# Long convolutions of a diffusion layer: full transforms by tables of both parities instead of radix 2, sums of absolute values on VectorE, and a fixed early order on TensorE

## The chip, the cores and the metric
The kernel runs on one core of one Trainium2 chip. The core's engines run their own instruction streams and wait for each other by semaphores: TensorE (PE; its weight loads are shown as PEld), VectorE (DVE), ScalarE (ACT), GpSimd (POOL) and SyncE (SP, which here only issues DMAs). The metric is the device time of one execution in microseconds; lower is better.

## What is computed
One layer of a diffusion backbone in float32: 512 latent tokens and 256 context tokens of width 1024. The part around the change is the Hyena branch, two long convolutions over the 512 positions with filters that a small network makes:

```python
def hyena_spectrum(n, w1, b1, w2, b2, w3, freq):
    ...
    h = jnp.sin(freq * (feats @ w1 + b1))
    h = jnp.sin(freq * (h @ w2 + b2))
    h = (h @ w3).reshape(n, 2, HY_ORDER, HY_W)
    ...
    filt = jnp.concatenate([h[:, 0], jnp.zeros((1, HY_ORDER, HY_W), f32), h[1:, 1][::-1]], axis=0)
    filt = filt / jnp.sum(jnp.abs(filt), axis=0, keepdims=True)
    return jnp.fft.rfft(filt, axis=0)

def hyena_mixer(u, sw, sb, spec, bias):
    u = short_conv(u, sw, sb)
    v, g1, g2 = jnp.split(u, HY_ORDER + 1, axis=-1)
    z = g1 * long_conv(v, spec[:, 0], bias[0])
    return g2 * long_conv(z, spec[:, 1], bias[1])
```

Before it, the modulation `c @ w_mod`, an RMS norm and the input projection `h @ w_in`; beside it attention and a Fourier branch; after it the merge of the three branches, routing, and 16 experts (SwiGLU, 64 tokens each), whose weights of 402 MB are the bulk of what is read.

## The kernel before
The kernel is written in a tile language. A planner orders the instructions of every engine by its own costs when the program is built, except in the stretch `early` (from L330 on), where `manual_schedule` keeps the order of the text on the engines that it names. The order on each engine is fixed in the program that runs. Values are kept in float32; for most matmuls a value is split into a high half (ScalarE copies it to the narrower format) and a low half (VectorE subtracts): `split`, L232 to 234. `mm3` (L227 to 230) multiplies two split values by three matmuls.

PSUM is given out as four buffers of 512 columns (`pmm`) and two pairs of them (`pbig`). Weights come through a ring of three 1 MB buffers (`load`, L224), issued on SP in order; a load waits until the matmuls on the buffer's old content are done.

The early stage (L330 to 513). SP loads the small network's weights, three of the eight tiles of `w_mod` (`wmods`), the decay table, x, the other five tiles as the ring comes free, then the context and the bias rows; GpSimd's queue loads the transform tables (`dfth`, `dftl`, L341; `invh`, `invl`, L598), which take half of the tile T2a. `mod1(kt)` is the modulation's matmul with tile kt into one PSUM buffer. `filt(t)` makes a quarter of the filters: matmuls, the product with the decay (L399), the split, absolute values on ScalarE (L405) in one buffer, and 16 matmuls per quarter that add them up in PSUM (`nsum`, L407). `xnorm` squares x on ScalarE (L380) and scales it on VectorE (L384). `spectra(f)` transforms the filters by planes (L228 to 230 with output `plane`; copies at L428, combinations L432 to 440), radix 2 over even and odd positions. `butterfly` (L448, L449) and `norms` (L502 to 512) finish the filters' spectra in `Gt`. The modulation row is copied at L486 and turned at L489. `need(idx)` splits a tile of `w_in`; `hT(i)` turns x and applies the modulation (L562, L564). The projections follow (`pj`, outputs `pmm`).

The convolutions (L644 to 870, 145 to 237 us in the trace). `forward` makes four half transforms of the tokens, odd and even positions apart, with 12 matmuls; ScalarE copies the odd ones (L653) and VectorE adds and subtracts (L655, L656) to give the planes `Zs` in SBUF. `pointwise(o, i)` multiplies both planes by the spectra (L666, L667), adds on VectorE for the real and mostly on GpSimd for the imaginary parts (L668, L669), undoes the radix 2 (L670, L671) and splits. The inverse transform of the first convolution takes 12 matmuls with 512 columns, that of the second, which gives channels by positions, 48 with 128 columns. Between them stand the projections 9 to 15 and the second part of the modulation (`mod2`, L790, 16 tiles through the same ring). In this part the planner orders all engines.

After the convolutions come attention with the rest of the projections as its filler, the merge, the routing (to about 560 us), and the experts, whose weights are prefetched into every buffer that comes free.

## Time and profile before

| | us |
|---|---|
| median of 3 runs | 1507.91 |
| lowest, highest | 1506.47, 1513.32 |
| the profiled execution | 1505.07 |
| its span, first to last instruction | 1503.3 |
| TensorE busy in the span | 1349.0 (90%) |
| VectorE busy | 514.5 (34%) |
| ScalarE busy | 286.2 (19%) |
| GpSimd busy | 134.7 (9%) |

The shares are averages over stages that have different limits, so the stages are read one by one, by windows of the trace. A row of the timeline gives the start, the length, the engine, the line of the kernel, the operation and the tiles (output <- inputs); in brackets the time that the engine stood idle before it and what ended that. Matmuls overlap: the distance of two starts, not the length, says what one costs.

### The profile page before, as it was taken

The page shows a single profiled execution, that of the slowest core. Times are in us where ns is not written, and L with a number is a line of the kernel's source. Part 1 is how long each engine was busy: PE and PEld are TensorE (multiplying, and loading weights), DVE is VectorE, ACT ScalarE, POOL GpSimd, SP SyncE. Part 2 cuts the span into 40 slices and gives each one's busy share as a digit, 9 for nine tenths or more (in the row PEclk, how much of TensorE's full clock was granted, in tenths as well). Part 3 has the DMA queues.
Part 4 walks back from the last instruction along what each step waited for, and adds up shares of the span by engine and source line. Part 5 has one row for each costly group of instructions (what it writes and reads, how often), then busy time and mean ns, then how long its engine had stood idle before and what let it go on. Part 6 is the DMA issues. An engine that isn't in the chain of part 4 may idle for free.

```text
span 1503.3 us, 16141 instructions
## 1 busy us (share of the span) xinstructions
PE 1349.0 (90%) x6681; PEld 718.5 (48%) x6681; DVE 514.5 (34%) x1010; ACT 286.2 (19%) x513; POOL 134.7 (9%) x128
## 2 busy tenths in 40 slices
PE   6899789999999889999999978979988989889896
PEld 3567458777788874433433423423423423423233
DVE  4676777667546471201211111101201201101123
ACT  4355224444433320100000000000000000000003
POOL 1033531000104110000000000000000000000002
PEclk8799899999999899999999999999999999999998
DMA  8414595311153766799999999999999999999994
GB/s 319 175 62 137 196 321 175 89 67 56 71 198 110 276 255 233 310 428 430 429 431 430 430 429 429 429 432 430 429 431 431 429 429 431 431 429 428 431 429 201
DMA packets 50371, 477.62 MB, mean 318 GB/s; under 512 B 5485, under 2 KB 10223, under 8 KB 16378
## 3 DMA queue, kind: packets, MB, share of 16 engines
q1 hardware_dynamic: 46008, 464.20, 75.1%
q0 software_dynamic: 2464, 8.00, 2.2%
...
q14 instruction: 21, 0.17, 0.0%
...
## 4 chain that ended last, share of the span: by engine, by line
PE 48%; DMA 39%; DVE 8%; ACT 2%; POOL 1%; issue 1%; SPq 0%; ACTq 0%; DVEq 0%; POOLq 0%
DMA rawT<-in_wu_dram 11%; DMA rawT3a<-in_wu_dram 9%; DMA rawwsp<-in_wg_dram 7%; PE py L1404 6%; PE pmm L228 6%; PE pmm L230 6%; PE pmm L229 6%; PE pu L1368 5%; PE pa L1368 5%; DMA rawT<-in_wd_dram 4%; PE gx L1339 3%; DMA rawT2a<-in_wg_dram 2%; DMA rawT2b<-in_wu_dram 2%; DMA rawwsp<-in_wu_dram 2%; PE pmm L1023 1%; PE pT L1010 1%
## 5 line engine op out<-in xcount | busy, mean ns | idle before, releaser
L1382 DVE TENSOR_TENSOR hid<-hid,pu 128x512 f32<-128x512 f32 x32 | 20.6, 684 | 455.6 <-PE pu L1368 443.2
L228 PE MATMUL pmm<-T,wsp 128*128 128x512 f32 x288 | 116.7, 408 | 4.2 <-ACT wsp L233 4.2
L230 PE MATMUL pmm<-T,wsp 128*128 128x512 f32 x288 | 114.6, 398 | 3.5 <-DVE wsp L234 3.5
L229 PE MATMUL pmm<-T,wsp 128*128 128x512 f32 x288 | 114.1, 396 | 0.0
L1381 ACT ACTIVATE hid<-pa 128x512 f32<-128x512 f32 x32 | 17.4, 594 | 419.6 <-PE pa L1368 405.2
L1324 POOL TENSOR_SCALAR vt<-iota,slot,rs 128x64 f32<-128x64 f32 x16 | 10.3, 669 | 735.5 <-PE stp L1419 717.0
L1339 PEld LDWEIGHTS gx<-vt,x 128*128 128x128 f32 x512 | 61.4, 193 | 29.3 <-issue 18.7
L1339 PE MATMUL gx<-vt,x 128*128 128x128 f32 x512 | 69.0, 287 | 5.2 <-DVE vt L1324 1.9
L1410 DVE TENSOR_TENSOR Y<-py,g2b 64x512 f32<-64x512 f32 x30 | 20.7, 689 | 152.6 <-PE py L1404 138.1
L234 DVE TENSOR_TENSOR wsp<-ld,wsp 128x1024 fp32r<-128x1024 f32 (+1 forms) x39 | 54.4, 1398 | 41.7 <-ACT wsp L233 41.6
L228 PEld LDWEIGHTS pmm<-T,wsp 128*128 128x128 f32 x288 | 54.7, 191 | 22.5 <-issue 7.0
L230 PEld LDWEIGHTS pmm<-T,wsp 128*128 128x128 f32 x288 | 54.8, 190 | 20.2 <-DVE wsp L234 5.0
L1404 PE MATMUL py<-rawT,hidT 128*64 128x512 f32 x224 | 50.6, 596 | 14.5 <-DMA rawT<-in_wd_dram 14.5
L1448 PE MATMUL sc<-Y,st 128*128 128x512 f32 (+1 forms) x128 | 57.0, 598 | 5.6 <-DVE Y L1410 5.6
L229 PEld LDWEIGHTS pmm<-T,wsp 128*128 128x128 f32 x288 | 55.0, 191 | 12.3 <-issue 1.7
L1390 ACT ACTIVATE hidT<-hp 128x512 f32<-128x512 f32 x16 | 9.6, 597 | 265.5 <-PE hp L1385 147.1
L233 ACT ACTIVATE wsp<-ld 128x1024 fp32r<-128x1024 f32 (+1 forms) x39 | 41.9, 1079 | 60.9 <-PE pmm L229 42.7
L1448 PEld LDWEIGHTS sc<-Y,st 128*128 128x128 f32 (+1 forms) x128 | 23.5, 189 | 39.5 <-issue 26.4
L1452 DVE TENSOR_TENSOR acc<-acc,sc 128x512 f32<-128x512 f32 x56 | 38.2, 686 | 10.9 <-PE sc L1448 10.9
L1404 PEld LDWEIGHTS py<-rawT,hidT 128*64 128x64 f32 x224 | 16.2, 137 | 48.6 <-issue 38.6
L1368 PE MATMUL pu<-rawT,xg 128*64 128x512 f32 x128 | 29.8, 597 | 9.8 <-DMA rawT<-in_wu_dram 9.8
L1368 PE MATMUL pu<-rawT,K1n 128*64 128x512 f32 x128 | 30.6, 599 | 6.8 <-DMA rawT<-in_wu_dram 6.8
(562 smaller groups left out, 2395.5 us busy)
## 6 DMA issues: line engine op xcount, KB each, us to landing
...
```

The lines of the kernel that those rows point to most:

```text
L228: mm(o, ah, bh, start=first, stop=False)
L229: mm(o, ah, bl, start=False, stop=False)
L230: mm(o, al, bh, start=False, stop=last)
L233: keep(A.activation(hi, src, AF.Copy))
L234: keep((eng or V).tensor_sub(lo, src, hi.bitcast(F32)))
L1339: mm(o[:, k % 4], x1[:, t, k * 128:(k + 1) * 128], oh[:, t], start=t == 0, stop=t == 3)
L1368: mm(ob[64 * hf:64 * hf + 64], xg[:, k, es_], w_[:, (2 * b + hf) * 512:(2 * b + hf + 1) * 512], start=k == 0, stop=k == 7)
L1382: V.tensor_mul(hid[:, bs], hid[:, bs], acc_[1][b] if e == NE - 1 else acc_[1][:, bs])
L1404: mm(o[64 * dh:64 * dh + 64, :], hcol(hT_, fb), w_[:, i * 1024 + dh * 512:i * 1024 + (dh + 1) * 512], start=fb == 0, stop=fb == 15)
L1410: V.tensor_mul(Y2[es2, dh * 512:(dh + 1) * 512], o[64 * dh:64 * dh + 64], M["g2b"][64 * dh:64 * dh + 64, dh * 512:(dh + 1) * 512])
L1448: mm(o, st[ks, t * 128:(t + 1) * 128], Y2[ks, ds_], start=True, stop=True)
L1452: V.tensor_add(acc[:, t, ds_], acc[:, t, ds_], o)
```

## The change
- **Tables.** The transform tables hold both parities: a second copy with the odd positions' sign turned (`e * [1, -1]`), so that each of the two planes f has its own table over all positions. The four tables grow from 256 KB to 512 KB each and fill T2a.
- **Transforms.** `forward(f)` makes plane f whole, by 12 matmuls that add even and odd positions in PSUM; its result stays in PSUM (two `pmm` buffers for plane 0, a `pbig` for plane 1). `pointwise(o, f, Z)` multiplies from there, for both halves i; the butterfly at its end is gone. `inverse(os_, f)` adds plane f's part of both outputs in PSUM, 12 matmuls per plane; the first plane's part is issued before the second plane's. The last inverse has 48 matmuls of 256 columns. `Zt` and the second T2b tile are gone. The filters' own spectra stay radix 2.
- **Absolute sums.** VectorE adds the quarters' absolute values in a tile `Fa`; `norms` sums over the partitions by two matmuls with ones and turns the result by four transposes. The `nsum` matmuls go.
- **Order.** `early` now covers TensorE too and reaches on to the first `need(0)`. Filters are made in the order 0, 2, 1, 3, between the modulation's matmuls, and the first two planes ahead of the last filter. win[0] is loaded right after the last tile of `w_mod`, ahead of the context. Half of x's scaling goes to ScalarE.

```diff
...
     e = np.stack([np.cos(ang), -np.sin(ang)], 2)
+    e = np.stack([e, e * np.array([1.0, -1.0])[:, None, None]], 3)
     c["dft_h"], c["dft_l"] = _split_const(e)
-    inv = e.transpose(3, 2, 1, 0) * (2.0 / 512.0)
+    inv = e.transpose(4, 3, 2, 1, 0) * (2.0 / 512.0)
     c["inv_h"], c["inv_l"] = _split_const(inv)
...
     Gt = hyg.tile([128, 2, 2, 2, 3, 256], F32, name="Gt")
-    dfth, dftl, invh, invl = (T2a[:, i, j].rearrange("p (a b f) -> p a b f", a=2, b=2) for j in (0, 2) for i in (0, 1))
+    dfth, dftl, invh, invl = (T2a[:, i, j:j + 2].rearrange("p a (b f n) -> p a b f n", b=2, f=2)
+                              for j in (0, 2) for i in (0, 1))
     B1 = cst.tile([128, 8, 2], F32, name="B1")
...
     early = scope()
-    early.enter_context(tc.manual_schedule(engines={ENG.SP, ENG.Activation, ENG.DVE}))
+    early.enter_context(tc.manual_schedule(engines={ENG.SP, ENG.Activation, ENG.DVE, ENG.PE}))
     packa = flat(E01)[:, :1667]
...
     wmods += [load(a["wmod"][kt * 128:(kt + 1) * 128, 0:2048]) for kt in range(3, 8)]
+    wst = {("ld", 0): load(a["win"][0])}
     xc = ep.tile([128, 2, 1024], F32, name="xc")
...
         for t in range(n):
-            V.tensor_scalar(xs[t0 + t], xs[t0 + t], r[:, t:t + 1], None, op0=OP.mult)
+            if t % 2:
+                A.activation(xs[t0 + t], xs[t0 + t], AF.Copy, scale=r[:, t:t + 1])
+            else:
+                V.tensor_scalar(xs[t0 + t], xs[t0 + t], r[:, t:t + 1], None, op0=OP.mult)
     Fh, Fl = ([flat(T3pair(x_, 2 * t)) for t in range(4)] for x_ in range(2))
     w3h, w3l = flat(T2b[:, 0, 1:3]), flat(T2b[:, 1, 0:2])
-    nsum = pmm("nsum")
+    Fa = ep.tile([128, 1024], F32, name="Fa")
     def filt(t):
...
         split(Ff, Fh[t], Fl[t])
-        Fa = flat(E10[:, 0:2])
-        A.activation(Fa, Ff, AF.Abs)
-        for b in range(8):
-            mm(nsum[:, b % 4:b % 4 + 1], Fa[:, b * 128:(b + 1) * 128], ones[:, 0:1], start=t == 0 and b == 0,
-               stop=t == 3 and b == 7)
+        if t:
+            Fb = flat(E10[:, 0:2])
+            A.activation(Fb, Ff, AF.Abs)
+            V.tensor_add(Fa, Fa, Fb)
+        else:
+            A.activation(Fa, Ff, AF.Abs)
     def plane(par, blk, dr, r):
         t = blk * 2 + par
-        mm3(o, dfth[:, par, r], dftl[:, par, r], Fh[t][:, dr * 512:(dr + 1) * 512], Fl[t][:, dr * 512:(dr + 1) * 512],
+        mm3(o, dfth[:, par, r, 0], dftl[:, par, r, 0], Fh[t][:, dr * 512:(dr + 1) * 512], Fl[t][:, dr * 512:(dr + 1) * 512],
             True, True)
...
         V.tensor_sub(hs_[os_, ns], h2_[gs], hs_[gs, ns].bitcast(F32))
-    early.close()
-    for kt in range(3):
-        mod1(kt)
+    mod1(0)
     filt(0)
+    mod1(1)
+    filt(2)
+    mod1(2)
     filt(1)
+    sp = spectra(0)
+    next(sp)
+    next(sp)
     mod1(3)
-    filt(2)
     filt(3)
-    mod1(4)
     xnorm(0, 4)
-    sp = spectra(0)
     for i in range(3):
         next(sp)
-        mod1(5 + i)
+        mod1(4 + i)
     drain(sp)
+    mod1(7)
     mrow = ep.tile([128, 512], F32, name="mrow")
...
     def norms():
-        nc_, ncol = (ep.tile([128, 4], F32, name=n) for n in ("nsc", "ncol"))
-        V.tensor_copy(nc_, nsum[:, :4])
-        V.reciprocal(ncol, nc_)
+        p_ = pmm("nsum")
+        for h in range(2):
+            mm(p_, ones, Fa[:, h * 512:(h + 1) * 512], start=h == 0, stop=h == 1)
+        V.tensor_mul(dbc, dbc, p_)
+        ns = ep.tile([128, 512], F32, name="mrow")
+        A.activation(ns, p_, AF.Copy)
+        p_ = pmm("ncol")
+        for b in range(4):
+            T.transpose(p_[:, b * 128:(b + 1) * 128], ns[:, b * 128:(b + 1) * 128], ident)
+        ncol = ep.tile([128, 4], F32, name="ncol")
+        V.reciprocal(ncol, p_[:, 0:512:128])
         V.tensor_tensor(sws, colp[:, C_SW + 8:C_SW + 24].rearrange("p (i j) -> p i j", i=4),
                         ncol[:, :, None].to_broadcast([128, 4, 4]), op=OP.mult)
-        dg = ep.tile([128, 1024], F32, name="dg", tag="Ft", bufs=3)[:, :512]
-        for b in range(4):
-            V.tensor_scalar(dg[:, b * 128:(b + 1) * 128], ident, nc_[:, b:b + 1], None, op0=OP.mult)
-        p_ = pmm()
-        mm(p_, ones, dg, start=True, stop=True)
-        V.tensor_mul(dbc, dbc, p_)
         G.tensor_add(Gt[:, :, 0, 0, 1, :], Gt[:, :, 0, 0, 1, :], v2(dbc))
-    wst = {}
     def need(idx):
...
         split(ht.rearrange("p (k n) -> p k n", k=2), hch[:, i:i + 2], hcl[:, i:i + 2])
+    early.close()
     need(0)
...
         return pb
-    def forward():
-        zo = pbig("planes")
-        ze = [pmm("plane") for _ in range(2)]
-        for par, zz in ((1, [zo[:, :512], zo[:, 512:]]), (0, ze)):
+    def forward(f):
+        Z = []
+        zb = pbig("planes") if f else None
+        for r in range(2):
+            z = zb[:, r * 512:(r + 1) * 512] if f else pmm("plane")
+            for m in range(2):
+                ms_ = slice(m * 512, (m + 1) * 512)
+                mm3(z, dfth[:, m, r, f], dftl[:, m, r, f], vh[:, ms_], vl[:, ms_], m == 0, m == 1)
+            Z.append(z)
+        return Z
+    def pointwise(o, f, Z):
+        for i in range(2):
             for r in range(2):
-                ps_ = slice(par * 512, (par + 1) * 512)
-                mm3(zz[r], dfth[:, par, r], dftl[:, par, r], vh[:, ps_], vl[:, ps_], True, True)
-        for r in range(2):
-            A.activation(Zs[1][r], zo[:, r * 512:(r + 1) * 512], AF.Copy)
-        for r in range(2):
-            V.tensor_add(Zs[0][r], ze[r], Zs[1][r])
-            V.tensor_sub(Zs[1][r], ze[r], Zs[1][r])
-    def pointwise(o, i):
-        for r in range(2):
-            e_ = G if r and (o, i) != (1, 1) else V
-            y = hyp.tile([128, 2, 256], F32, name="cvy", bufs=2)
-            for f in range(2):
                 t0 = hyp.tile([128, 512], F32, name="cv0", bufs=2)
                 t1 = hyp.tile([128, 512], F32, name="cv1", bufs=2)
-                V.tensor_mul(t0, Zs[f][0], flat(Gt[:, o, f, r, 1 - i:3 - i, :]))
-                V.tensor_mul(t1, Zs[f][1], flat(Gt[:, o, f, 1 - r, 1 - i:3 - i, :]))
+                V.tensor_mul(t0, Z[0], flat(Gt[:, o, f, r, 1 - i:3 - i, :]))
+                V.tensor_mul(t1, Z[1], flat(Gt[:, o, f, 1 - r, 1 - i:3 - i, :]))
+                e_ = G if r and (o, f, i) != (1, 1, 1) else V
                 e_.tensor_tensor(t0, t0, t1, op=OP.add if r else OP.subtract)
-                e_.tensor_tensor(y[:, f], t0[:, :256], t0[:, 256:], op=OP.add)
-            e_.tensor_tensor(y[:, 1], y[:, 0], y[:, 1], op=OP.subtract)
-            V.scalar_tensor_tensor(y[:, 0], y[:, 0], 2.0, y[:, 1], op0=OP.mult, op1=OP.subtract)
-            for m in range(2):
-                split(y[:, m], Yh[m][:, r, i * 256:(i + 1) * 256], Yl[m][:, r, i * 256:(i + 1) * 256], e_)
+                y = hyp.tile([128, 256], F32, name="cvy", bufs=2)
+                e_.tensor_tensor(y, t0[:, :256], t0[:, 256:], op=OP.add)
+                split(y, Yh[f][:, r, i * 256:(i + 1) * 256], Yl[f][:, r, i * 256:(i + 1) * 256], e_)
+    def inverse(os_, f):
+        for m in range(2):
+            for r in range(2):
+                mm3(os_[m], invh[:, f, r, m], invl[:, f, r, m], Yh[f][:, r], Yl[f][:, r], f + r == 0, f + r == 2)
     qscr = tc.dram_tile([64, 2, 8, 512], F32, name="qscr")
...
     g1t = hyp.tile([128, 1024], F32, name="g1t")
-    Zt = big2.tile([128, 2, 4, 512], F32, name="Zt", tag="T2b")
-    Zs = [[Zt[:, f, r] for r in range(2)] for f in range(2)]
-    forward()
-    pointwise(0, 0)
+    Z = forward(0)
+    pointwise(0, 0, Z)
     mod2(2)
     o = proj(9)
+    Z = forward(1)
     short_conv(uV1[:, 1], o, 3)
-    pointwise(0, 1)
+    pointwise(0, 1, Z)
     mod2(2)
             A.activation(g1t, to_tokens(uV1), AF.Copy)
+            oz = [pmm(), pmm()]
+            inverse(oz, 0)
         u_ = hyp.tile([128, 512], F32, name="uf", bufs=2)
...
         mod2(2)
+    inverse(oz, 1)
     for m in range(2):
-        o = pmm()
-        for r in range(2):
-            mm3(o, invh[:, r, m], invl[:, r, m], Yh[m][:, r], Yl[m][:, r], r == 0, r == 1)
         z = hyp.tile([128, 512], F32, name="zt")
-        V.tensor_mul(z, o, g1t[:, m * 512:(m + 1) * 512])
+        V.tensor_mul(z, oz[m], g1t[:, m * 512:(m + 1) * 512])
         split(z, vh[:, m * 512:(m + 1) * 512], vl[:, m * 512:(m + 1) * 512])
     o = proj(12)
-    forward()
+    Z = forward(0)
     short_conv(uG[:, 0], o, 4)
-    pointwise(1, 0)
+    pointwise(1, 0, Z)
     mod2(2)
     o = proj(13)
+    Z = forward(1)
     short_conv(uG[:, 1], o, 5)
-    pointwise(1, 1)
+    pointwise(1, 1, Z)
     mod2(4)
...
     q_stack(0, 1)
-    T2b = big2.tile([128, 2, 4, 512], F32R, name="T2b", tag="T2b")
     for c in range(2):
             cs_ = slice(i * 256 + c * 128, i * 256 + (c + 1) * 128)
-            for m in range(2):
-                os_ = slice(i * 256 + m * 128, i * 256 + (m + 1) * 128)
+            for f in range(2):
                 for r in range(2):
-                    mm3(o[:, os_], Yh[m][:, r, cs_], Yl[m][:, r, cs_], invh[:, r, m], invl[:, r, m], r == 0, r == 1)
+                    mm3(o[:, i * 256:(i + 1) * 256], Yh[f][:, r, cs_], Yl[f][:, r, cs_], flat(invh[:, f, r]), flat(invl[:, f, r]),
+                        f + r == 0, f + r == 2)
         z = hyp.tile([128, 512], F32, name="zt")
```

## Rows read from the trace of the kernel before
**Rows 1.** The page's chain that ended last, whole span, share by engine.
```profile
PE 48%; DMA 39%; DVE 8%; ACT 2%; POOL 1%; issue 1%; SPq 0%; ACTq 0%; DVEq 0%; POOLq 0%
```

**Rows 2.** The chain in order of time: start us, length us, what.
```profile
50.19 2.75 DVE xa L384 x4
...
187.10 1.85 PE pmod L790 x16
...
783.02 32.98 DMA rawT<-in_wu_dram
```

**Rows 3.** Windows: us, busy us of each engine (instructions), clock, DMA share, GB/s.
```profile
61.00:145.00 84.00, 79.75 (x374) 58.78 (x372) 58.69 (x82) 46.05 (x67) 26.20 (x19) 0.99 0.32 98
...
145.00:237.30 92.30, 77.44 (x397) 49.95 (x397) 72.63 (x116) 24.25 (x40) 35.46 (x32) 0.93 0.73 244
...
170.00:175.00 5.00, 0.00 (x0) 0.00 (x0) 5.00 (x8) 1.81 (x3) 2.10 (x3) 0.74 0.48 187
...
640.00:680.00 40.00, 38.65 (x177) 13.19 (x174) 3.35 (x5) 1.68 (x3) 0.00 (x0) 1.00 1.01 429
```

**Rows 4.** Who TensorE waited for, 145 to 237.3 us: us, times, longest.
```profile
PE pmm L228 <- ACT T3a L233: 8.6, 1, 8.6
...
PE pmod L790 <- DMA ld<-in_wmod_dram: 3.6, 3, 2.8
```

**Rows 5.** Timeline of TensorE: start us, length us, engine, line; neighbours' starts give the step.
```profile
90.28 0.28 PE L228 MATMUL pbig<-T2b,wsp 128*128 128x256 f32 x1
...
90.40 0.28 PE L229 MATMUL pbig<-T2b,wsp 128*128 128x256 f32 x1
...
90.52 1.02 PE L510 MATMUL pmm<-dg,ones 128*128 128x512 f32 x2
...
183.54 0.39 PE L228 MATMUL pmm<-T,wsp 128*128 128x512 f32 x1
...
183.77 0.39 PE L229 MATMUL pmm<-T,wsp 128*128 128x512 f32 x1
...
234.71 0.28 PE L229 MATMUL pmm<-T2a,T3b 128*128 128x128 f32 x1
...
234.82 0.27 PE L230 MATMUL pmm<-T2a,T3b 128*128 128x128 f32 x1
```

**Rows 6.** Groups on VectorE, 145 to 237.3 us: busy us, mean ns.
```profile
L666 DVE TENSOR_TENSOR cv<-Zt,Gt 128x512 f32<-128x512 f32 x16 | 13.7, 854 | 1.3 <-POOL cvy L669 1.3
...
L671 DVE SCALAR_TENSOR_TENSOR cvy<-cvy 128x256 f32<-128x256 f32 x8 | 3.9, 486 | 3.7 <-POOL cvy L670 3.6
...
L655 DVE TENSOR_TENSOR Zt<-plane,Zt 128x512 f32<-128x512 f32 x4 | 2.7, 688 | 1.0 <-PE plane L230 1.0
```

**Rows 7.** Timeline of VectorE and GpSimd side by side in the first convolution.
```profile
158.08 3.54 POOL L668 TENSOR_TENSOR cv<-cv,cv 128x512 f32<-128x512 f32 x1 [13.05 <-DVE cv L667]
...
159.46 0.68 DVE L667 TENSOR_TENSOR cv<-Zt,Gt 128x512 f32<-128x512 f32 x1
...
160.40 0.74 DVE L632 SCALAR_TENSOR_TENSOR uG<-pmm,sws,uG 128x511 f32<-128x511 f32 x1
...
167.35 1.21 DVE L666 TENSOR_TENSOR cv<-Zt,Gt 128x512 f32<-128x512 f32 x1
```

**Rows 8.** TensorE's group of absolute sums, 0 to 62 us.
```profile
L407 PE MATMUL nsum<-ones,E 128*128 128x1 f32 x64 | 10.6, 296 | 3.0 <-ACT E L405 3.0
```

**Rows 9.** Timeline of the early stage, 12 to 62 us.
```profile
18.51 2.36 DVE L399 TENSOR_TENSOR Ft<-pbig,E 128x1024 f32<-128x1024 f32 x2 [1.81 <-PE pbig L396]
...
32.58 1.23 DVE L234 TENSOR_TENSOR T3b<-Ft,T3b 128x1024 fp32r<-128x1024 f32 x1 [3.52 <-ACT T3b L233]
...
34.62 1.06 ACT L405 ACTIVATE E<-Ft 128x1024 f32<-128x1024 f32 x1 [2.08 <-PE nsum L407]
...
49.69 0.60 ACT L486 ACTIVATE mrow<-mod 128x512 f32<-128x512 f32 x1 [5.24 <-PE mod L362]
...
60.31 0.79 PE L230 MATMUL pmm<-T,wsp 128*128 128x512 f32 x1 [1.15 <-DVE wsp L234]
```

## The prediction
> **What bounds the kernel now.** First the page's chain that ended last [rows 1]: TensorE holds 48% of the span and DMA 39%. The chain in order of time says when [rows 2]: through TensorE and VectorE up to 783 us, from there mostly through the expert weights' DMA. The windows say why [rows 3]: from 640 us the DMA engines are busy all the time, at 429 GB/s, with a fixed amount of weights still to bring. Their buffers come free as TensorE works off the stages before. So a microsecond gained or lost on the path before 640 us moves the end by one, and what the change does after that is nothing. I therefore price two stages: the early one (0 to 62 us) and the two long convolutions (145 to 237.3 us).
>
> The second window of [rows 3] is the convolution stage: 92.3 us long, TensorE busy 77.4, VectorE 72.6. Neither is full, because they wait for each other: from 170 to 175 us TensorE does nothing at all while VectorE is busy throughout. The waits name the reason [rows 4]: 8.6 us in one piece for the last spectrum of the pointwise products (ScalarE's half of the split that VectorE feeds), and 3.6 us for modulation weights. After such a hole TensorE's steps are slow for some time. How much is lost altogether I get from the work at full clock. A 512-column matmul takes a step of 0.23 us, a 128-column one 0.11 [rows 5], a tile of modulation weights 0.93, with the gap behind it 1.0 [rows 2]. In the stage stand 7 projections of 24 (168 x 0.23 = 38.6), 16 modulation tiles (16.0), 24 forward (5.5), 12 first inverse (2.8), 48 short ones of the last inverse (5.3), 16 transposes (1.8): 70.0 us. 22.3 us are lost.
>
> **The convolutions, part by part.** Added on TensorE: each forward transform goes from 12 to 24 matmuls, twice (24 x 0.23 = 5.5); the first inverse from 12 to 24 (2.8); the last inverse keeps 48, but of 256 columns at 0.12 instead of 128 at 0.11 [rows 5] (0.5). Together +8.8, none of it hidden where TensorE is the bound.
>
> Removed on VectorE [rows 6]: 8 sums and differences of forward (L655 and L656, 8 x 0.69 = 5.5), 8 of L671 (3.9), and 5 of L670, which has their shape (5 x 0.49 = 2.4); 11.8 of 72.6 us. GpSimd loses 3 of L670. The count of products, L668, L669 and splits stays. The products now read the spectrum from PSUM: the PSUM-reading L655 takes 0.688 us [rows 6], a product left in peace 0.68 [rows 7], so I take zero; bounds: -0.17 each (L666's mean of 0.854 down to 0.688, 32 of them, -5.3 us) and +0.05 (+1.6).
> [...]
>
> More than sizes, the order changes. Plane 0's products need only forward(0), without the copies and butterflies, and inverse(oz, 0) needs only plane 0. TensorE has the projections 9 to 11, six modulation tiles, forward(1) and inverse(oz, 0), some 31 us, to lay over VectorE's two planes. The new balance is 70.0 + 8.8 = 78.8 us of TensorE against 61 us of VectorE. What stays lost: the stage from 61 to 145 us [rows 3] has a like balance (VectorE 58.7 beside TensorE 79.8 of 84.0) and TensorE idle 4.2 of it, 5%; 5% of 79 is 4.0; the 3.6 us for modulation weights stay (the ring of three loads isn't touched); some 0.9 for the clock after them. 8.5 in all. Bounds: 3.6 (the weights alone) and 22.3 (nothing goes). New stage: 78.8 + 8.5 = 87.3, **-5.0 us**, from -9.9 to +8.8. PSUM: plane 0's spectrum holds two of four "mm" buffers until its products are done, and plane 1's holds the free "big" pair, so to_tokens waits for plane 1's products. Behind that stand the g1t copy and the product zt, which need the last split anyway: zero, at most 2 us, inside the upper bound.
>
> **The early stage.** The 64 matmuls of absolute sums go: 10.6 us busy and 3.0 waiting [rows 8]. They share one buffer with ScalarE's absolute values, which wait for them in turn, 2.08 us before the last [rows 9]. That row of waits holds back the planes and the modulation matmuls behind it on TensorE; the modulation row is copied only at 49.7 [rows 9]. But in its place comes a row on VectorE, since all four engines now keep the program's order: per filter a product (about 1.2), ScalarE's high half (1.05), the low half (1.23 [rows 9]) and the sum of absolutes (about 1.23), one after another: 4.8 us. From the first product (18.5 [rows 9], and 2 later because the tables double, below) four filters end at 20.5 + 3.6 + 0.5 + 3 x 4.8 = 39.0. Then ScalarE squares x (four of 1.05 and their sums, 5), the reciprocal root and the scaling follow (4): x is scaled at some 47, where before it was at 53 [rows 2]. In the other strand the sixth plane waits for a PSUM buffer that ScalarE's copy or VectorE's first combination frees, and both stand behind that scaling; behind the plane stand the matmuls of modulation 5 to 7 and, by the ring, the load of win[0]; the ctx load and the bias rows stand behind that on SP (they have 20 us in hand). I get a modulation row at 52 to 55 in place of 49.7, win[0] split at 56 to 60, and projections that flow from 58 to 61; before, they flowed from 60.3, when the low half of the weights came [rows 9]. Value **-1.5 us**; bounds -6 (x alone decides) and +5 (the modulation row alone decides). The tables: four of 512 KB for 256 KB, so 1 MB more, which at the 429 GB/s of [rows 3] delays what queues beside them by up to 2.4 us, counted above.
>
> **The rest.** norms: two full-precision matmuls and four transposes for one matmul of 1.02 us [rows 5]: +0.5 to +1.5, or nothing if they land in an early hole of TensorE; +0.7. Half of x's scaling on ScalarE is inside the 4 us above; removing Zt frees no one.
>
> **Sum**: -5.0 - 1.5 + 0.7 = -5.8. The profiled execution took 1505.1 us (span 1503.3), so 1499.3; the median of the runs shown is 2.8 above that execution, so 1502 for the median.
>
> **Rivals.**
> A, the forecast (0.42): most of the wait goes, 1502; own range 1496 to 1508.
> B, everything goes (0.28): plane 0's inverse and forward(1) fill every hole, only the weights' 3.6 us stay, and early x decides: -9.9 - 4 = -14, so 1494. For it: VectorE and GpSimd hinder each other today. L668 on GpSimd took 3.54 us beside VectorE's products, and a product 1.21 beside GpSimd [rows 7]; which of the two is held up changes, as the product of 0.68 shows. The PSUM-reading L632 took 0.74 beside the same GpSimd instruction. With spectra in PSUM the 32 products would leave that conflict. Against: the adds and splits stay in SBUF.
> [...]
> C, no change (0.16): the hole only moves (TensorE's order in the convolutions is the planner's, and it may put to_tokens or the inverse too early again), about half of the 22 us stays and the early stage gives 5 back: 1506 to 1510.
> D, slower (0.14): the added 8.8 us fall on a TensorE that still ends its wait at the last split. Place: inverse(oz, 1) and the second forward pair. It decides from a remaining loss of 21 us on, near today's 22.3, and gives +8.8 + 0.7 and no early gain: 1517. Against it: VectorE has 12 us less to do before that split.
> That the change doesn't do what it says (plane 0's inverse issued only behind the last split) is a form of D or C.
>
> **How the numbers follow.** A measurement can tell about 0.5%, 7.5 us, from no change. Faster than 1500.4: B and the lower third of A, 0.40. Within: the rest of A and C, 0.46. Slower: D, 0.14. Range 1490 to 1514: it leaves out D and a little of B.
>
> **What would show it.** Convolution stage near 87 us, TensorE busy over 90% of it, the 8.6 us wait gone, VectorE's products at 0.69 with no long ones beside GpSimd; no absolute-sum matmuls; x scaled near 47 but the modulation row after 50; projections flowing near 59. The forecast is wrong if TensorE still stands for over 5 us before an inverse, if the early stage ends over 4 us from today's, or if the stages in between move.

## The result and the profile after

The changed kernel takes 1493.9 us (median; 1492.1 to 1495.6) against 1510.6 before (the three executions of the table and a fourth): ratio 0.989, 95% interval 0.986 to 0.992. Measured again later, on one chip with both, it is 1493.9 against 1509.9: 0.989 (0.988 to 0.991). The forecast of 1502, with its range from 1490 to 1514, had the sign right; its change of -5.8 us is about a third of that between the medians (-16.7). The profiled executions differ by less than the medians, 1505.1 us before and 1494.5 after, so -10.6; of that it is over half.

I cut each trace at two instructions that every kernel has: the first transpose of to_tokens (the convolutions start) and the first product with the fc weights (behind the last inverse). From the kernel before, and then from the changed one, TensorE's timeline (start us, length us, line, operation):
```profile
142.81 1.11 PE L640 MATMUL pbig<-packb,uT 128*128 128x128 f32 x8
...
245.12 0.36 PE L228 MATMUL pmm<-fc,T3b 128*128 128x256 f32 x1 [0.82 <-DMA fc<-in_fc_h_dram]
```
```profile
142.82 1.11 PE L650 MATMUL pbig<-packb,uT 128*128 128x128 f32 x8
...
235.28 0.35 PE L229 MATMUL pmm<-fc,T3b 128*128 128x256 f32 x1 [0.27 <-DMA fc<-in_fc_h_dram]
```
So in these two executions the early part is equal, the convolutions go from 102.3 to 92.5 us (-9.9), and what follows lasts 1258.2 and 1257.4. The chain that ended last has the same shape as [rows 1]:
```profile
PE 50%; DMA 41%; DVE 6%; ACT 2%; issue 1%; POOL 0%; SPq 0%; ACTq 0%; DVEq 0%
```
The same stretch as a window of each kernel (busy us of PE, PEld, DVE, ACT, POOL with their counts, then granted clock, DMA share, GB/s), before and after; the third row is after's counterpart of the convolution window of [rows 3]:
```profile
142.81:245.12 102.31, 85.99 (x439) 56.76 (x438) 77.86 (x124) 31.15 (x49) 39.44 (x38) 0.93 0.75 250
```
```profile
142.82:235.28 92.46, 89.72 (x476) 61.78 (x474) 66.79 (x100) 28.77 (x45) 34.83 (x38) 1.00 0.79 277
...
142.90:228.00 85.10, 82.62 (x445) 56.20 (x444) 63.91 (x96) 23.59 (x38) 32.58 (x34) 1.00 0.77 273
```
TensorE has more work and nearly no gap (2.7 us idle where it was 16.3), VectorE 11 us less, and the mean granted clock is 1.00 where it was 0.93. The 8.6 us wait of [rows 4] is gone. In this stretch TensorE waits for loads alone:
```profile
PE pmod L798 <- DMA ld<-in_wmod_dram: 2.5, 3, 1.7
PE pmm L229 <- DMA fc<-in_fc_h_dram: 0.3, 1, 0.3
```
Nor does the first inverse wait for its input any more. Its last split in the kernel before, then in the changed one, and there the start of the inverse of plane 0 and of that on the last split:
```profile
184.29 0.73 POOL L234 TENSOR_TENSOR T3a<-cvy,T3a 128x256 fp32r<-128x256 f32 x1
```
```profile
173.99 0.73 POOL L235 TENSOR_TENSOR T3b<-cvy,T3b 128x256 fp32r<-128x256 f32 x1 [0.53 <-ACT T3b L234]
...
174.66 0.48 PE L229 MATMUL pmm<-T3a,T2a 128*128 128x512 f32 x1
...
179.43 0.50 PE L229 MATMUL pmm<-T3b,T2a 128*128 128x512 f32 x1
```
With the same start of the stretch the last split ends at 174.7 and not at 185.0, 10.3 us earlier, and the inverse on it comes 4.7 us behind it. (The wait of 8.6 us before was for an earlier split of the same chain, done at 177.7.) In every trace of the old convolutions that split ends 41.7 to 42.2 us into the stretch, in every one of the new ones without an edit to them 31.9 to 32.3.

The products of VectorE, now from PSUM, are all near 0.68 us, where [rows 6] has 0.854 for L666 (groups: busy us, mean ns):
```profile
L673 POOL TENSOR_TENSOR cv<-cv,cv 128x512 f32<-128x512 f32 x7 | 9.8, 1404 | 31.6 <-DVE cv L671 31.6
...
L670 DVE TENSOR_TENSOR cv<-plane,Gt 128x512 f32<-128x512 f32 x8 | 5.5, 683 | 0.1
...
L671 DVE TENSOR_TENSOR cv<-planes,Gt 128x512 f32<-128x512 f32 x8 | 5.4, 676 | 0.0
```
The long products beside GpSimd are gone, but some of what still reads two SBUF operands got longer, as the low halves of the spectra's splits, before and after:
```profile
L234 DVE TENSOR_TENSOR T3a<-cvy,T3a 128x256 fp32r<-128x256 f32 x5 | 2.1, 414 | 0.0
```
```profile
L235 DVE TENSOR_TENSOR T3a<-cvy,T3a 128x256 fp32r<-128x256 f32 x4 | 3.6, 909 | 0.0
```
The early part after the change, beside [rows 9] (timeline):
```profile
43.88 1.42 DVE L390 TENSOR_SCALAR xa<-xa,xr 128x1024 f32<-128x1024 f32 x2
...
46.01 0.79 PE L229 MATMUL plane<-T3b,T2a 128*128 128x512 f32 x1 [10.35 <-DVE Gt L441]
...
54.15 0.60 ACT L495 ACTIVATE mrow<-mod 128x512 f32<-128x512 f32 x1 [7.12 <-PE mod L365]
...
60.52 0.50 PE L230 MATMUL pmm<-T,wsp 128*128 128x512 f32 x1 [1.31 <-DVE T L235]
```
x is scaled by 46 us and not by 53, but the sixth plane stands 10.35 us behind that scaling, the modulation row comes at 54.2 (49.7 before), and the projections flow from 60.5 (60.3 before).

All kernels by the two cuts, each read from the same two rows of its own trace ("rest" is the span less the second cut). Medians and ratios go over all timed executions. The kernel before was timed again beside each group, and its own median differs by 2 us between the groups; so where two kernels come from different groups, a distance of 2 us between their medians says nothing.

| kernel | to-tokens at | convolutions | rest | median | ratio to before (95%) |
|---|---|---|---|---|---|
| before | 142.8 | 102.3 | 1258.2 | 1508.6 to 1510.6 | 1 |
| before, again | 141.7 | 102.5 | 1258.3 | (1504.2) | |
| after | 142.8 | 92.5 | 1257.4 | 1493.9 | 0.989 (0.986 to 0.992) |
| after, again | 141.4 | 92.7 | 1258.0 | 1493.9 | 0.989 (0.988 to 0.991) |
| convolutions alone | 150.1 | 92.2 | 1257.8 | 1502.8 | 0.997 (0.995 to 0.998) |
| early half alone | 138.4 | 102.1 | 1257.6 | 1501.7 | 0.996 (0.995 to 0.998) |
| sums alone | 134.3 | 102.0 | 1259.1 | 1497.2 | 0.991 (0.990 to 0.992) |
| planes copied | 140.6 | 97.8 | 1258.1 | 1499.2 | 0.993 (0.990 to 0.996) |
| inverse late | 140.0 | 91.8 | 1257.8 | 1493.3 | 0.991 (0.989 to 0.993) |
| one term more | 141.0 | 95.6 | 1260.7 | 1497.3 | 0.992 (0.990 to 0.995) |
| modulation first | 143.1 | 92.6 | 1257.9 | 1495.3 | 0.993 (0.990 to 0.995) |
| TensorE kept busy | 139.0 | 92.7 | 1258.4 | 1492.1 | 0.989 (0.986 to 0.991) |
| planes first | 138.5 | 92.7 | 1257.2 | 1490.6 | 0.987 (0.986 to 0.988) |
| planes first, busy | 137.5 | 98.6 | 1258.0 | 1495.4 | 0.989 (0.988 to 0.991) |

### The profile page after: what moved, and what is told of

It is laid out like the page before. It is cut to its first block, busy times and chain, and to the rows that moved or that the text cites. A ratio compares the mean times of both kernels' runs of the same rounds, so it can differ in the third digit from the quotient of the medians.

```text
span 1492.7 us, 16055 instructions
## 1 busy us (share of the span) xinstructions
PE 1347.9 (90%) x6659; PEld 715.2 (48%) x6659; DVE 501.0 (34%) x981; ACT 287.8 (19%) x513; POOL 129.3 (9%) x128
## 4 chain that ended last, share of the span: by engine, by line
PE 50%; DMA 41%; DVE 6%; ACT 2%; issue 1%; POOL 0%; SPq 0%; ACTq 0%; DVEq 0%
DMA rawT<-in_wu_dram 11%; DMA rawT<-in_wd_dram 7%; DMA rawT3a<-in_wu_dram 6%; PE py L1410 6%; PE pmm L229 6%; PE pmm L230 6%; PE pmm L231 6%; PE pu L1374 6%; PE pa L1374 5%; DMA rawwsp<-in_wg_dram 5%; DMA rawwsp<-in_wu_dram 5%; PE gx L1345 2%; DMA rawT2a<-in_wg_dram 2%; DMA rawT2b<-in_wu_dram 2%; PE pmm L1029 2%; PE pT L1016 1%
## 5 line engine op out<-in xcount | busy, mean ns | idle before, releaser
L1330 POOL TENSOR_SCALAR vt<-iota,slot,rs 128x64 f32<-128x64 f32 x16 | 10.3, 670 | 735.5 <-PE stp L1425 716.8
L1416 DVE TENSOR_TENSOR Y<-py,g2b 64x512 f32<-64x512 f32 x30 | 20.7, 689 | 155.9 <-PE py L1410 141.4
L235 DVE TENSOR_TENSOR wsp<-ld,wsp 128x1024 fp32r<-128x1024 f32 (+1 forms) x39 | 54.5, 1406 | 41.5 <-ACT wsp L234 41.3
L231 PEld LDWEIGHTS pmm<-T,wsp 128*128 128x128 f32 x288 | 54.2, 188 | 16.1 <-DVE wsp L235 2.6
```

Source lines behind the costliest of these rows:

```text
L231: mm(o, al, bh, start=False, stop=last)
L235: keep((eng or V).tensor_sub(lo, src, hi.bitcast(F32)))
L1416: V.tensor_mul(Y2[es2, dh * 512:(dh + 1) * 512], o[64 * dh:64 * dh + 64], M["g2b"][64 * dh:64 * dh + 64, dh * 512:(dh + 1) * 512])
```

## The experiments

**The convolutions alone.** The forward, pointwise and inverse functions and their tables as in the change; the early half as before.
```diff
-    forward()
-    pointwise(0, 0)
+    Z = forward(0)
+    pointwise(0, 0, Z)
...
+    Z = forward(1)
...
+            inverse(oz, 0)
...
+    inverse(oz, 1)
```


> The convolution half of the change alone (full transforms by tables of both parities, products from PSUM, the inverse in two halves); the early half stays as before: sums on TensorE, the planner's order. Theory (the whole gain is made in the convolution stage and carried 1:1 to the end): the stage from 142.9 us to the mark that stood at 237.3 before and 228.0 after becomes 85 to 86 us (94.4 before), the profiled execution is 9 to 10 us under that of before, and the medians agree with the changed kernel within 3 us. Rival (the early half brings 5 to 6 us that the two profiled executions do not show, since the medians differ by 16.7 us and the profiled executions by 10.6): the stage is as short, but the median lies 5 us or more above that of the changed kernel.

1502.8 us, 5.8 under before. TensorE's timeline:
```profile
150.05 1.11 PE L642 MATMUL pbig<-packb,uT 128*128 128x128 f32 x8
...
242.27 0.36 PE L229 MATMUL pmm<-fc,T3b 128*128 128x256 f32 x1 [0.57 <-DMA fc<-in_fc_h_dram]
```
The convolutions are as short as in the changed kernel (92.2), so their gain is theirs alone. But the early part is 7 to 8 us longer than in either trace of before, although its code is the same but for the larger tables, and its instructions on TensorE come in the same order. Its timeline shows where that begins:
```profile
21.32 1.22 DVE L401 TENSOR_TENSOR Ft<-pbig,E 128x1024 f32<-128x1024 f32 x1 [4.61 <-PE pbig L398]
...
40.51 3.58 PE L409 MATMUL nsum<-ones,E 128*128 128x1 f32 x16 [1.21 <-ACT E L407]
...
55.28 2.74 DVE L386 TENSOR_SCALAR xa<-xa,xr 128x1024 f32<-128x1024 f32 x4
```
The first filter's product comes 2.8 us later than in [rows 9], as TensorE waited 2.1 us for early modulation weights (0.5 before) and then ran the filters at a granted clock of 0.87 and 0.70 (16 to 20 and 20 to 24 us; 1.00 in both before). The last row of sums starts 4.8 us later (35.73 before), and x is scaled 5.1 us later than in [rows 2]. So a small delay at the start grew along the sums. It starts with the 1 MB more of tables: the decay table, loaded beside them, lands 16.9 to 17.9 us after its issue in all ten traces with the larger tables and 14.8 to 15.2 in the four with the smaller ones. How much of the 7 to 8 us that is, no run with the tables alone tells. The rival held for the time: the changed kernel lies 8.9 us lower, nearly all of it ahead of to-tokens.

**The early half alone.** Fixed TensorE order, sums on VectorE, scaling shared, win[0] placed; the convolutions as before.
```diff
-    early.enter_context(tc.manual_schedule(engines={ENG.SP, ENG.Activation, ENG.DVE}))
+    early.enter_context(tc.manual_schedule(engines={ENG.SP, ENG.Activation, ENG.DVE, ENG.PE}))
...
+            V.tensor_add(Fa, Fa, Fb)
```


> The early half alone (TensorE order of the filters fixed by hand, absolute sums added by VectorE, two of the four x tiles scaled by ScalarE, win[0] loaded where the order puts it); the convolutions stay as before. Theory (the early half is worth nothing: the modulation row comes at 54 us instead of 49.7, and the projections start at 60.3 to 60.5 us either way): to-tokens starts at 142.5 to 143.5 us, the convolution stage stays at 94 to 95 us, and the median is within 2 us of that of before. My prediction's early step: -1.5 us, between -6 and +5. Rival (the early half holds the 6 us between the medians and the profiled pair): 5 us or more under before.

1501.7, 6.9 under before: my theory fell. To-tokens starts at 138.4, 3.3 and 4.4 us earlier than in the two traces of before. The sixth plane waits in this trace too:
```profile
44.16 0.79 PE L228 MATMUL plane<-T3b,T2a 128*128 128x512 f32 x1 [10.35 <-DVE Gt L439]
```
With the larger tables the same early half starts to-tokens at 140.0 to 142.8 in five traces (after, after again, planes copied, inverse late, one term more), 1.6 to 4.4 us later. So the early half is worth 6 to 7 us in the median with the smaller tables, although it has the hole.

**The sums alone.** The kernel before; only the absolute sums go from TensorE to VectorE.
```diff
-        for b in range(8):
-            mm(nsum[:, b % 4:b % 4 + 1], Fa[:, b * 128:(b + 1) * 128], ones[:, 0:1], ...)
+        if t:
+            Fb = flat(E10[:, 0:2])
+            A.activation(Fb, Ff, AF.Abs)
+            V.tensor_add(Fa, Fa, Fb)
```


> The kernel before, with one piece of the early half alone: the absolute sums added by VectorE and summed by two matmuls at the end, instead of 64 small matmuls beside the filters. TensorE's order stays the planner's, x is scaled by VectorE, win[0] is loaded as before, the convolutions are those of before. The whole early half gave 6.9 us in the medians. Theory (it is the fixed order that counts: filters, planes and modulation no longer interleaved with gaps at half clock): within 2.5 us of the kernel before. Rival (it is the sums: 10.6 us of TensorE at small matmuls, gone): 4 to 7 us under the kernel before.

1497.2, 12.7 under before in the medians (in the traces to-tokens comes 7.4 and 8.5 us earlier), and some 5 us under the whole early half: the theory that the order counts fell, and the rival was too low. One row of the kernel before, then the timeline of this one:
```profile
39.56 0.80 PE L228 MATMUL plane<-T3a,T2a 128*128 128x512 f32 x1 [0.25 <-DVE nsc L502]
```
```profile
39.91 2.73 DVE L384 TENSOR_SCALAR xa<-xa,xr 128x1024 f32<-128x1024 f32 x4
...
43.27 0.60 ACT L487 ACTIVATE mrow<-mod 128x512 f32<-128x512 f32 x1 [7.10 <-PE mod L362]
...
51.79 0.79 PE L230 MATMUL pmm<-T,wsp 128*128 128x512 f32 x1 [1.15 <-DVE wsp L234]
```
x is scaled by 42.6 (53 before, 46 after), the modulation row comes at 43.3 (49.7, 54.2), and the projections flow from 51.8 (60.3, 60.5). In the planner's order the planes and the modulation go on while x is squared. So the sums were the price of the old early part, in two ways that no run separates. They stood in TensorE's queue, waited for ScalarE (3.0 us, [rows 8]), and everything behind waited with them. And they held one of the four PSUM buffers to their end: before, the third plane waits for it until 39.56 (the row above), while here three planes are done by 27.5. The rest of the early half (fixed order, shared scaling, win[0]) takes some 5 us of that back on the old convolutions. The sums with the new convolutions and the planner's order weren't run; from the two parts (1497.2, and 9.9 us of convolutions) that is an estimated 1487, later by what the larger tables cost at the start.

**Modulation first.** The last 16 modulation matmuls ahead of the remaining planes.
```diff
+    mod1(4)
+    mod1(5)
+    mod1(6)
+    mod1(7)
     xnorm(0, 4)
-    for i in range(3):
-        next(sp)
-        next(sp)
-        mod1(4 + i)
     drain(sp)
-    mod1(7)
```


> The changed kernel, with the last four steps of the modulation (16 matmuls) put ahead of the remaining spectrum planes in TensorE's fixed order, so that they run while the planes wait for their PSUM buffers. Theory (the sixth plane waits 10.35 us behind the scaling of x, and the modulation, its row, the load of win[0] and its split are queued behind that plane; this is where the early half loses what it gains by the earlier scaling): the modulation row comes at 45 to 49 us (54.15 in the changed kernel), projections flow from 53 to 56 us (60.5), and the whole is 4 to 7 us under the changed kernel. Rival (the loads of the projections' weights, not the row, set when the projections can flow, or the planes that now come later hold up the Gt chain and the first conv): the row is early, but to-tokens starts within 1.5 us of 143.0, and the whole is within 1.5 us of the changed kernel.

1495.3, no better than the changed kernel: the rival held. The row came at 47.7 and the projections flow from 55.95 (60.5 in the changed kernel, after two single products at 57.6). But TensorE did nothing from 52 to 55.95 except its transposes, and what came then ran at half clock (windows):
```profile
52.00:56.00 4.00, 0.98 (x9) 0.74 (x7) 4.00 (x8) 1.07 (x4) 0.00 (x0) 0.93 0.18 29
56.00:62.00 6.00, 6.00 (x16) 4.49 (x17) 4.92 (x17) 2.40 (x3) 0.00 (x0) 0.50 0.39 157
```
By 62 us it had finished 10 products of the projections, the changed kernel 7, and by 70 us 34 against 33: the lead was nearly gone.

**TensorE kept busy.** 38 matmuls into an unread PSUM buffer where the sixth plane waits.
```diff
+    wm = pbig("warm")
     for i in range(3):
         next(sp)
+        if i == 1:
+            for _ in range(38):
+                mm(wm[:, :512], dfth[:, 0, 0, 0], Fh[0][:, :512], start=True, stop=True)
         next(sp)
         mod1(4 + i)
```


> The changed kernel, with 38 matmuls of 512 columns into a PSUM buffer that nobody reads, put into TensorE's order where the sixth spectrum plane waits (36 to 46 us, no matmul at all from 36 to 44 us, granted clock 0.78 then 0.50 until 52 us). 38 x 0.23 = 8.7 us at full clock, double that at half clock. Theory (the early half loses time because TensorE, after such holes, does its next work at half clock): the clock stays near 1.00 from 36 to 52 us, planes and modulation behind the hole take 4 to 5 us instead of 7, to-tokens comes 2 to 4 us earlier, the time is 2 to 4 us under the changed kernel. Rival (the stretch behind the hole waits for the x tiles and for win[0], whatever the clock): within 1 us of the changed kernel. Point against: if the extra matmuls run at half clock they end at 52 us, and all is 4 to 6 us later.

1492.1, by ratio and median 0.6 to 1.9 us under the changed kernel, within its interval, so between the theory's 2 to 4 and the rival's 1: the mechanism shows, and a gain in time isn't clear of the noise. Windows of the changed kernel, then of this one:
```profile
36.00:44.00 8.00, 0.00 (x0) 0.00 (x0) 4.42 (x15) 5.49 (x10) 0.00 (x0) 0.64 0.32 122
44.00:52.00 8.00, 5.99 (x17) 2.86 (x17) 3.44 (x5) 3.03 (x4) 2.50 (x2) 0.50 0.19 46
```
```profile
36.00:44.00 8.00, 8.00 (x37) 6.61 (x36) 4.15 (x13) 5.74 (x10) 0.00 (x0) 1.00 0.41 131
44.00:52.00 8.00, 6.06 (x36) 2.31 (x35) 4.41 (x8) 3.31 (x5) 2.52 (x2) 1.00 0.31 97
...
51.84 0.60 ACT L499 ACTIVATE mrow<-mod 128x512 f32<-128x512 f32 x1 [4.44 <-PE mod L365]
```
Without the hole the granted clock is 1.00 in both windows, 33 useful matmuls and the last 3 unread ones fit from 44 to 52 us where 17 did at 0.50, and the row comes 2.3 us earlier, though the plane could start no earlier (46.38 against 46.01).

**Planes first.** The remaining planes and the modulation ahead of the squares and the scaling of x.
```diff
-    xnorm(0, 4)
     for i in range(3):
         next(sp)
         next(sp)
         mod1(4 + i)
     drain(sp)
     mod1(7)
+    xnorm(0, 4)
```


> The changed kernel, with the whole rest of the first spectrum's planes and the modulation ahead of the squares and the scaling of x, on TensorE, VectorE and ScalarE. Theory (the sixth plane then no longer waits behind the scaling): no wait of 10 us on TensorE there, the modulation row at 42 to 46 us (54.15 in the changed kernel), x scaled 1 to 2 us later (47 to 48.5), projections from 51 to 55 us (60.5), and TensorE idle ahead of them, so that their first 5 to 8 us run at half clock: the time 1 to 4 us under the changed kernel. Rival (as in the run with the modulation first: all that is gained goes to the clock): within 1 us or up to 3 us over the changed kernel.

1490.6, 3.3 under the changed kernel beside it, as the theory had it (1 to 4), and the lowest median of the study; all its four executions lie under all eight of the changed kernel. The wait for the sixth plane is gone and x is scaled from 45.2, little over a microsecond later than in the changed kernel. TensorE is done with the modulation at 43.2, but the row is copied only at 47.32, as ScalarE has the squares and the scaling ahead of it (a miss of my 42 to 46). Projections from 53.1. The granted clock is 0.79 in the mean from 52 to 60 us; matmuls of 512 columns that follow each other step by 0.24 to 0.31 us up to 54.5, by 0.41 to 0.43 from there to 57.7, and by 0.23 to 0.24 from 59.3. So half clock came, but for an estimated 3 us (by these steps) and not the 5 to 8 that I expected:
```profile
47.95 1.11 PE L498 MATMUL pmm<-packb,mrow 128*128 128x128 f32 x4 [4.77 <-ACT mrow L495]
...
53.11 0.73 PE L229 MATMUL pmm<-T,wsp 128*128 128x512 f32 x2 [2.35 <-DVE ht L573]
...
52.00:60.00 8.00, 6.89 (x28) 5.38 (x29) 6.47 (x20) 2.40 (x5) 0.00 (x0) 0.79 0.49 198
```

**Planes first, and TensorE kept busy.**
```diff
     xnorm(0, 4)
+    wm = pbig("warm")
+    for _ in range(32):
+        mm(wm[:, :512], dfth[:, 0, 0, 0], Fh[0][:, :512], start=True, stop=True)
```


> As the run with the planes first, and 32 matmuls of 512 columns into a PSUM buffer that nobody reads (32 x 0.23 = 7.4 us at full clock) behind the modulation, where TensorE has nothing to do until x is scaled. Theory (the clock is what the order alone loses): granted clock 0.95 to 1.00 from 40 to 61 us, projections at full clock from their start, to-tokens at 133 to 137 us (142.8 and 140.0 in profiles of the changed early half), the time 4 to 7 us under the changed kernel. Rival (x or win[0] come last whatever the clock): within 1.5 us of the run with the planes first.

1495.4, worse than with the planes first. The early part did what was expected in kind (clock 1.00 from 40 to 61 us, to-tokens at 137.5, 1.1 us earlier than with the planes first and just outside the 133 to 137 expected). What was lost came later: the convolutions took 98.6 us. TensorE's waits in this stretch, then the window from 200 to 220 us here and with the planes first:
```profile
PE pmod L801 <- DMA ld<-in_wmod_dram: 6.5, 3, 3.7
...
200.00:220.00 20.00, 14.59 (x65) 8.57 (x58) 13.85 (x22) 3.08 (x6) 6.09 (x8) 0.83 1.01 289
```
```profile
200.00:220.00 20.00, 18.20 (x104) 12.31 (x105) 16.66 (x24) 4.66 (x8) 6.43 (x9) 1.00 0.96 305
```
The instructions of the stretch come in the same order in both kernels, but TensorE waited 6.5 us for modulation weights (2.3 with the planes first), with the DMA engines busy throughout at a lower rate (289 GB/s against 305), and the granted clock in that window was 0.83 against 1.00. Of this kernel's five executions two took 1490.5 and 1490.8 us, as with the planes first, and three 1495.4 to 1497.5: so it seems not to happen each time, though only one of them has a trace. Why the weights come late is open; neither theory covers it.

**Planes copied.** Each spectrum plane copied by ScalarE to SBUF ahead of its products.
```diff
+            A.activation(Zs[f][r], z, AF.Copy)
-            Z.append(z)
+            Z.append(Zs[f][r])
```


> The changed kernel, with each spectrum plane copied by ScalarE to SBUF (8 copies of 128x512) before the products, so that the 32 products of VectorE read SBUF instead of PSUM; order and TensorE work stay. The products took 854 and 813 ns from SBUF before and 676 to 683 ns from PSUM after; GpSimd's sum of them 1886 before and 1404 ns after. Theory (reading PSUM keeps VectorE's products out of the way of GpSimd, and that is what shortened both): products at 0.80 to 0.86 us, the GpSimd sum at 1.8 to 1.9 us, the stretch from to-tokens to the first fc product 2 to 5 us longer (92.4 after), the time 2 to 5 us over the changed kernel. Rival 1 (the products are shorter for another reason): they stay near 0.68 us, and only the copies' wait is added, 0 to 2 us. [...]

1499.2, 5.3 over the changed kernel; the stretch is 5.4 longer. Groups, TensorE's waits, and one product beside one sum on GpSimd:
```profile
L672 DVE TENSOR_TENSOR cv<-Zt,Gt 128x512 f32<-128x512 f32 x16 | 13.3, 848 | 1.7 <-POOL cv L674 1.2 <-ACT Zt L662 0.5
L671 DVE TENSOR_TENSOR cv<-Zt,Gt 128x512 f32<-128x512 f32 x16 | 12.7, 816 | 0.2 <-ACT Zt L662 0.2
L674 POOL TENSOR_TENSOR cv<-cv,cv 128x512 f32<-128x512 f32 x7 | 10.6, 1507 | 32.1 <-DVE cv L672 32.1
...
PE planes L229 <- ACT Zt L662: 3.6, 2, 2.8
...
151.64 1.33 POOL L674 TENSOR_TENSOR cv<-cv,cv 128x512 f32<-128x512 f32 x1 [8.52 <-DVE cv L672]
...
151.74 1.78 DVE L672 TENSOR_TENSOR cv<-Zt,Gt 128x512 f32<-128x512 f32 x1
```
The same pair in the changed kernel:
```profile
153.26 1.34 POOL L673 TENSOR_TENSOR cv<-cv,cv 128x512 f32<-128x512 f32 x1 [7.88 <-DVE cv L671]
...
153.36 0.68 DVE L671 TENSOR_TENSOR cv<-plane,Gt 128x512 f32<-128x512 f32 x1
```
With the operand back in SBUF the mean product is back at 0.82 to 0.85 us: it was the place of the operand that shortened them. But these means mix two kinds. A product that no GpSimd instruction overlaps takes 0.68 to 0.69 us from SBUF too. Of the 15 that one overlaps, 7 take 1.2 to 1.8 us; in the kernel before it is 8 of 11 (0.77 to 1.76), and the other three ran beside the two longest sums on GpSimd (3.54 and 2.33 us), which were then the ones held up. From PSUM all 32 take 0.67 to 0.69, 16 of them beside GpSimd. GpSimd's sum rises only from 1.40 to 1.51 us in the mean, not to the 1.8 I expected; sums as long as those two don't come back. The copies cost 3.6 us of the 5.4 directly, as TensorE waits for them before it may write the next plane. It waits for no product: the last split ends 35.9 us into the stretch (31.9 in the changed kernel) and the inverse on it starts at 38.7. So the longer products can hold at most the other 1.8. Four products read each plane, and the copy still loses. Beside GpSimd a product took 0.67 to 0.69 us with one operand in PSUM, up to 1.8 with both in SBUF.

**The first inverse late.** Its first half issued just ahead of the second.
```diff
-            oz = [pmm(), pmm()]
-            inverse(oz, 0)
...
+    oz = [pmm(), pmm()]
+    inverse(oz, 0)
     inverse(oz, 1)
```


> The changed kernel, with the first half of the first inverse (the 12 matmuls of spectrum plane 0) moved from beside the modulation matmuls to just ahead of the second half. The same work, only later on TensorE. Theory (the first half fills a stretch in which TensorE would wait for the products of plane 1; a matmul triple of 512 columns takes 3 x 0.23 us at full clock): TensorE has 12 matmuls, 2.8 us, more behind the last products, and that comes on top of the stage: +2 to +3 us over the changed kernel. Rival (the last products are not what the inverse waits for, TensorE is full anyway, so the order does not matter): within 0.5 us of the changed kernel in the stage.

The stretch is 91.8 us, the time 1493.3: the 2 to 3 us of the theory don't come, and the rival is nearer. But the edit moves little. The planner orders this part, and already in the changed kernel it issues plane 0's inverse at 174.66, behind the three projections, six modulation tiles and forward(1) and 4.8 us ahead of the second half; here it starts 1.2 us later in the stretch and 4.1 us ahead. So the run can't price an early inverse. That plane 0's inverse can be done early isn't what filled the hole: the changed kernel doesn't do it early.

**One term more.** 16 more matmuls in the forward transforms.
```diff
+                mm(z, dftl[:, m, r, f], vl[:, ms_], start=m == 0, stop=False)
-                mm3(z, dfth[:, m, r, f], dftl[:, m, r, f], vh[:, ms_], vl[:, ms_], m == 0, m == 1)
+                mm3(z, dfth[:, m, r, f], dftl[:, m, r, f], vh[:, ms_], vl[:, ms_], False, m == 1)
```


> The changed kernel, with the fourth term of the split product (low table by low data) added to every forward transform: 16 more matmuls of 512 columns, 16 x 0.23 = 3.7 us of TensorE, nothing else. It tells whether added TensorE work is paid in full, as the sum of the prediction took it (8.8 us added, all on the path). Theory (after the change TensorE is the bound of the convolution stage, with 2 to 4 us of idle left): the stretch from to-tokens to the first fc product is 3 to 4 us longer than 92.4, and the time is 3 to 4 us over the changed kernel. Rival (VectorE's chain is still the bound, TensorE waits for it): 0 to 1 us.

The stretch is 95.6 us, 3.1 more, and the median 3.4 more, of 3.7 us of added work. (In this trace what follows the stretch is longer too, 1260.7 against 1257.4 and 1258.0; why is open, so I go by the stretch.) TensorE is the bound of this stage now, and added work is paid nearly in full. The 8.8 us that the change adds are therefore real, and what it removed is an estimated 8.8 + 9.9, some 19 us, of gaps and of matmuls at a lower clock. The windows bear that out: TensorE's idle time falls by 13.6 us, and its busy time grows by 3.7 for 8.8 of work, so some 5 us less at a lower clock (0.93 in the mean before, 1.00 after). In the kernel before, matmuls of 512 columns behind the 8.6 us wait came at steps of 0.42 to 0.43 us from 178.3 to 182.6 us and of 0.22 to 0.24 from 182.85 on; its windows there:
```profile
175.00:180.00 5.00, 2.26 (x5) 1.82 (x6) 5.00 (x6) 1.52 (x3) 3.54 (x4) 0.50 0.00 0
180.00:185.00 5.00, 5.00 (x18) 3.98 (x17) 2.29 (x3) 0.83 (x2) 4.39 (x4) 0.74 0.62 205
```

**The kernel before and the changed one, again.**

> The kernel before, unchanged, profiled a second time. In the profiles so far the stretch from to-tokens to the first fc product is the same for the same convolutions within 0.8 us (102.3 and 102.1 us with the old ones; 92.5, 91.8, 92.6 and 92.2 with the new ones), while the time at which to-tokens starts differs for the same early code: 142.8 and 140.0 (new early half), 142.8 and 150.1 (old one), and the granted clock between 20 and 61 us with it. Theory (the profiled execution of the kernel before had a good early half by chance; its early half takes 145 to 150 us in most executions, and the new early half is 4 to 7 us shorter): to-tokens at 145 to 150 us, the stretch after it 102 to 102.5. Rival (142.8 is usual, the old early half was only slow beside the new convolutions): 142 to 143.5.

> The changed kernel once more, unchanged, beside the kernels of this call on the same chip. Theory (the executions of one kernel differ in the early half alone): to-tokens at 139 to 143 us, the stretch from there to the first fc product 92.0 to 92.8 us, the rest 1257 to 1258.5 us, median 1492 to 1495. Rival (the stretch or the rest differ as well): one of them by more than 1 us.

The convolutions (102.5 and 92.7) repeat within 0.2 us of the first traces, the rest (1258.3 and 1258.0) within 0.6; the early part moves by 1.2 and 1.5 us. For the kernel before the theory fell: to-tokens at 141.7, earlier than in the first trace, so no trace of it shows the 145 us or more that I expected of most executions. For the changed kernel all four numbers of the theory held.
```profile
141.66 1.11 PE L640 MATMUL pbig<-packb,uT 128*128 128x128 f32 x8
...
244.13 0.35 PE L228 MATMUL pmm<-fc,T3b 128*128 128x256 f32 x1 [1.01 <-DMA fc<-in_fc_h_dram]
```

## Why the prediction was right in sign and short in size

**The profiled execution** was to be 1499.3 and was 1494.5, 4.8 less. Nearly all of it is one term (4.9 too little there, 0.8 too much in the early part, and 0.8 less behind the second cut, which I had at nothing).

**Convolutions, -5.0 forecast, -9.9 measured** (just at the bound; by the windows of [rows 3] 92.3 to 83.0 us, -9.3, and 0.6 more between the last inverse and the fc products). The work counted on TensorE was right: the added 8.8 us are paid (one term more). The long wait went. Mis-sized was the residual loss. I took 8.5 us, 4.0 of it by analogy with the stage from 61 to 145 us, and 0.9 for the clock that no row gave and no run shows (the granted clock was 1.00 in the changed kernel's stretch). In the changed kernel's own window it is 85.1 us less 2.1 (its start lies that far ahead of the one of [rows 3]), so 83.0, less 78.8 of work: 4.2, near the bound of the weights alone (3.6; the waits show 2.5). The analogy put idle time into a stage in which TensorE, once it was the bound, waited for nothing but weights.

That VectorE lost 11 us for my 11.8 is luck. What I struck out made 11.3. The products, which I had at zero, gave 4.9 more (26.7 to 21.8, near the bound of -5.3), since those beside GpSimd are no longer held up (0.67 to 0.69 us, where they took up to 1.76); no row gave the +0.05 us each of the other bound, and no run shows it. But the conflict moved: the low halves of the spectra's splits went from 4.8 to 7.1 us and the 256-wide sums from 4.1 to 5.1.

The argument by order holds in the main: TensorE lays the projections 9 to 11, six modulation tiles and forward(1) over VectorE's two planes, as I wrote, where before only two projections and two matmuls of the third stood ahead of the inverse. Plane 0's inverse isn't part of it, as it comes behind them. The other half is the chain of VectorE and GpSimd, 10.3 us shorter up to the last split. With the copies, and the products from SBUF, 4.0 us of that are lost (planes copied) and TensorE still doesn't wait for the split; so the operands in PSUM alone don't explain it. How the rest divides between the work struck out and the products by planes, no run separates.

**Early part and norms, -0.8 forecast, 0.0 between the first two traces**, and -0.3 between the second two. Step by step it went as written: x scaled at 46 (forecast 47; the terms given add up to 48), the row at 54.2 (52 to 55), projections from 60.5 (58 to 61). What I didn't see is that this was the price of the fixed order and no consequence of moving the sums: the sums alone bring the row to 43.3. I had named the sixth plane's wait behind the scaling, priced it, and not asked whether the planes need to stand there; the run with planes first moves them and gains 3.3 us. The larger tables were priced well, up to 2.4 us: by the middle of the traces the decay table lands some 2.3 us later.

**From the execution to the median.** I carried over that the median of before lies 2.8 above its profiled execution. More executions put it 3.5 to 5.5 above the 1505.1 of that one (1508.6 to 1510.6), and the second profiled one, of 1504.2, lies 5.1 under its group: both draws were low. The changed kernel's median lies 0.6 below its first profiled execution and 0.1 above its second. So the medians differ by 16, of which the traces of these two kernels show 10. The other 6 match in size what the early half brings by itself in the medians (6.9), and the early part is the only one of the three that moves by over a microsecond between traces of one kernel. But no trace of before holds a long early part, and with the larger tables the early half's traces lose part of its gain; so that the 6 us lie there is argued and not shown. The clock goes along with the time: of the 22 executions of before timed with the first four experiments, the two shortest spans (1498.9 and 1500.3 us) have a mean granted clock of 0.978 and 0.976, and the five with the lowest clock (0.969 and 0.970) are 1507.1 to 1509.7 long; the changed kernel's clocks are 0.979 to 0.984. It isn't strict (the two longest, 1510.7 and 1511.0, have 0.972 and 0.974), and it doesn't say which of the two is the cause.

**The rivals.** B (1494) came out in the time, in part by luck, as it counted from a median of 1507.9 and not 1510.6. Its mechanism is half there: the conflict of VectorE and GpSimd is real (beside GpSimd, 15 of 26 products from SBUF took 0.77 to 1.8 us, all from PSUM 0.67 to 0.69), and the holes filled, though not by plane 0's inverse; its early gain of 4 us is in neither pair of traces of the two kernels. C and D needed a stall ahead of the inverse that did not return.
